# Activation halves side by side, a start offset for the weights, and two matmuls in place of three in the feed-forward part

## The chip, the cores and the metric

The kernel runs on one core of one Trainium2 chip. The metric is the device time of one execution in microseconds. Before the change it is 1631.69 us, the median of three runs (1628.85 to 1634.49).

## The reference

One token sequence of 256 positions and 2048 channels goes through two blocks in fp32. The first has a gated chunk attention and a linear recurrence between two large projections. The second has pooling, latent attention and attention to a memory, and ends in a gated feed-forward part with a short causal convolution over the positions. That last part is what matters here:

```
def conv_glu_ffn(h, w_gate, w_up, conv_w, conv_b, w_down):   # h: 256 x 2048
    g = h @ w_gate                                            # 2048 x 5632
    gp = jnp.pad(g, ((0, 0), (CONV_WIDTH - 1, 0), (0, 0)))
    gc = conv_b
    for j in range(CONV_WIDTH):
        gc = gc + conv_w[j] * gp[:, j:j + S]
    return (jax.nn.silu(gc) * (h @ w_up)) @ w_down            # 5632 x 2048
```

## The kernel before

Activations stand transposed: 128 channels on the partitions, 256 positions (T) along the row. Each fp32 operand of a large product is split into a rounded part and the rest, both as fp32r ("hi" and "lo"). A product is the sum of three matmuls: hi by hi, hi by lo, lo by hi.

Weights come by DMA in tiles of 1 MB (`load`, three buffers `wr`) and are split on the chip by `split_w`: ScalarE writes the high part `wh` (L114, three buffers), VectorE the rest `wl` (L115, two buffers), four 128-row slices at a time where the tile is 256 columns wide. What `split_w` gives is one job of `tile_mm`. A job is put in a short queue (`submit`, one job deep in the feed-forward phase), so that the split of the next job is issued before the matmuls of this one. After its matmuls a job takes steps from the queue of evacuations (`drain`); in the feed-forward phase the budget is 0.1, so one step with a cost is taken per job.

`one` issues the matmuls of one block, a 128 x 128 piece of weights. In mode "T" the weights are the stationary operand and an activation row of 256 positions is the moving one:

```
trip = ((hi[:, s], xh), (hi[:, s], xl), (lo[:, s], xh))
for i, (l, r) in enumerate(trip):
    PE.matmul(o, l, r, start=st and i == 0, stop=sp and i == 2, skip_group_check=True)
```

Two neighbouring blocks share one PSUM bank of 512 columns. In mode "N" the activations are stationary and 512 (or 384, 320) weight columns move.

The feed-forward part takes 22 pairs j of 256 gate and 256 up columns, each with 16 slices of 128 channels and two blocks per slice: 22 x 2 x 16 x 2 = 1408 blocks, four jobs of 8 blocks for gate and four for up. `ev_gate` scales a bank by R3 (L1275), convolves (L1279 to L1281) and applies silu (L1284, L1285). `ev_up` multiplies (L1300) and splits into the tile `f` (L119, L120). Then `w_down` follows, 8 groups x 44 slices x 2 = 704 blocks, with `ev_out` adding the bank to the residual (L1320) and sending it out (L1321). `h1`, `h2` and `h3` hold the normalised inputs of the large products, with all high halves in front of all low halves; `y` tiles hold the mixers' outputs as separate tiles for high and low, `s1` to `s4` the halves of the memory.

Tiles are placed one behind the other in steps of 32 bytes. By that count the weight tiles `wr`, `wh` and `wl` start at byte 32 modulo 128 in each partition, `h` at 0, `y`, `f`, `s1` to `s4` and `qlH` at 96, `kvH` at 0.

Of the kernel before, what the change touches and what calls it, by code (L numbers as in the profile page):

```python
# [17 lines left out]
P = 128  # L18
T = 256
# [39 lines left out]
def trunk_kernel(ctx, tc, a, out):  # L59
# [74 lines left out]
    def tile_mm(src, kc0, kt, cw, mode, banks, act, first, last, pre=None, post=None):  # L134


        raw = load(src, kt, cw)
        n = 2 if mode == "N" else cw // P
        nk = 4 if cw == 256 else 2

        def one(kc, b, hi, lo):
            xh, xl = act(kc0 + kc)
            hi, lo = hi[:, kc % nk, :], lo[:, kc % nk, :]
            st, sp = first and kc == 0, last and kc == kt - 1
            if mode == "T":
                o = banks[b // 2][:, (b % 2) * T : (b % 2) * T + T]
                s = slice(b * P, b * P + P)
                trip = ((hi[:, s], xh), (hi[:, s], xl), (lo[:, s], xh))
                st = st and b % 2 == 0
            else:  # L150
                o = banks[b][:, :cw]
                s = slice(b * P, b * P + P)
                trip = ((xh[:, s], hi), (xh[:, s], lo), (xl[:, s], hi))
            for i, (l, r) in enumerate(trip):
                PE.matmul(o, l, r, start=st and i == 0, stop=sp and i == 2, skip_group_check=True)  # L155
# [127 lines left out]
    def ytile(tag, dt=F32):  # L283
        return yp.tile([P, 8, T], dt, tag=tag, name=tag)

    xt = [ytile("yL0"), ytile("yL1")]
    ada_raw = [ytile(t).rearrange("p (k a) t -> p k (a t)", k=4) for t in ("yH0", "yH1")]
# [126 lines left out]
    def make_h(j):  # L414
        if not h1:
            h = hpool.tile([P, 2, DC, T], F32R, tag="h", name="h1")
            h1.extend((h[:, 0], h[:, 1]))
        V.scalar_tensor_tensor(gs[:, 4 * j : 4 * j + 4], modT[:, 16 + 4 * j : 20 + 4 * j], 1.0,
                               colr("norm_g", 4 * j, 4), ALU.add, ALU.mult)
        for k in range(4 * j, 4 * j + 4):  # L420
            x, H, L, sh = xt[k // 8][:, k % 8, :], h1[0][:, k, :], h1[1][:, k, :], modT[:, k : k + 1]
# [4 lines left out]
    acth = lambda kc: (h1[0][:, kc, :], h1[1][:, kc, :])  # L426

    def front():
        steps = ada_steps((4, 0), ("VVVV", "VPPP"))
        for i, n in enumerate(FRONT):  # L430
# [14 lines left out]
            (lambda kg: a["w_mem_kv"][1, kg], 512, "N", ev_memv)], range(4), lambda kc: (mH(kc), mL(kc)),  # L445
# [350 lines left out]
    def after(kg, n, banks, ng, mode, dst, g, fin):  # L796
        for i, b in enumerate(banks):
            later(0.6, lambda i=i, b=b: part(kg, ng, mode, dst, g, b, i, fin), evq)
        if n == 0:
            steps.append(ada_steps((4 + kg + 1, kg + 1), PAIR) if kg < 3 else gates)  # L800
        if (n % 4 < EARLY and (kg < 3 or n >= GSTART)):
            next(steps[-1], None)
        if kg == 1 and n == 2:
            load_masks()
        if kg == 3 and n == 3:
            when(("in8", "in9", "in10", "in11"), recurrence_inputs)
        if kg == 3 and n in (8, 11):
            i = (n - 8) // 3
            when((f"aq{4 * i}", f"aq{4 * i + 2}", f"ak{4 * i}", f"ak{4 * i + 2}", f"in{4 + i}"), lambda: chunk_heads(i))
        if kg < 3 and n == 11:  # L810
            for _ in steps[-1]:
                pass
            make_h(kg + 1)
            if kg == 2:
                hgt.extend((ytile("yH0"), ytile("yL0")))
# [36 lines left out]
    acty = lambda kc: tuple(t[:, kc % 8, :] for t in y[kc // 8])  # L852

    def gate(src, z, h, k):
        V.tensor_tensor(src[:, h, :], src[:, h, :], z[0][:, h, :], ALU.mult)
        if h == 0:
            y[k // 8] = tuple(ytile(f"{t}{k // 8}", F32R) for t in ("yH", "yL"))
        split(src[:, h, :], *acty(k))
        done.add(f"y{k}")
# [22 lines left out]
    x1s, h2, sq1, pools = [], [], [], []  # L882

# [3 lines left out]
    def ev_x1(g):  # L887
        def one(i, b):
# [3 lines left out]
            gsplit(j, "g_mix", x1s[0][:, j, :], h2[0][:, j, :], h2[1][:, j, :])  # L892
# [9 lines left out]
    def need_y(kg):  # L902
# [6 lines left out]
        if kg == 1 and not xp:  # L909
# [11 lines left out]
            h = hpool.tile([P, 2, DC, T], F32R, tag="h", name="h2")  # L921
            h2.extend((h[:, 0], h[:, 1]))
# [6 lines left out]
    x1, (h2H, h2L) = x1s[0], h2  # L929
# [15 lines left out]
    act2 = lambda kc: (h2H[:, kc, :], h2L[:, kc, :])  # L945
    two = lambda b: b.rearrange("p (a b) -> p a b", a=2)
# [9 lines left out]
    y2p, y2m = ytile("yL0", F32R), ytile("yL1", F32R)  # L956
    y2pH, y2pL, y2mH, y2mL = y2p[:, 0:4, :], y2p[:, 4:8, :], y2m[:, 0:4, :], y2m[:, 4:8, :]
# [146 lines left out]
    y2H, y2L = ytile("yH0", F32R), ytile("yH1", F32R)  # L1104
# [93 lines left out]
    actq = lambda kc: (qlH[:, kc, :], qlL[:, kc, :])  # L1198
    actkv = lambda kc: (kvH[:, kc, :], kvL[:, kc, :])
# [10 lines left out]
    def acty2(kc):  # L1210
        if kc < 4:
            return y2pH[:, kc, :], y2pL[:, kc, :]
        if kc < 12:
            return y2H[:, kc - 4, :], y2L[:, kc - 4, :]
        return y2mH[:, kc - 12, :], y2mL[:, kc - 12, :]

    h3, sq2 = [], []

    def ev_x2(g):
        def one(i, b):  # L1220
            if not h3:
                h = hpool.tile([P, 2, DC, T], F32R, tag="h", name="h3")
                h3.extend((h[:, 0], h[:, 1], h))
                sq2.append(s2("pab", [P, 8, T]))
            s = slice(4 * g + 2 * i, 4 * g + 2 * i + 2)
            V.tensor_tensor(x1[:, s, :], two(b), x1[:, s, :], ALU.add)
            for j in range(s.start, s.stop):
                gsplit(j, "g_ffn", x1[:, j, :], h3[0][:, j, :], h3[1][:, j, :])
                done.add(f"f{j}")
# [30 lines left out]
    def open_f():  # L1260
# [9 lines left out]
    act3 = lambda kc: (h3[0][:, kc, :], h3[1][:, kc, :])  # L1270

    def ev_gate(j, sg):
        def start(b, gp):
            G.memset(gp[:, :, 0:2], 0.0)  # L1274
            V.tensor_tensor(gp[:, :, 2:], two(b), bc(R3, 2), ALU.mult)  # L1275
# [11 lines left out]
        def ev(banks):  # L1287
# [3 lines left out]
            later(0.8, lambda: start(banks[0], gp), evq)  # L1291
# [5 lines left out]
    def ev_up(j, sg):  # L1297
        def one(b):
            t = tmp([P, 2, T], "ub")
            V.tensor_tensor(t, two(b), sg[0], ALU.mult)  # L1300
            split(t, f[j][:, 0], f[j][:, 1])

        def ev(banks):
            later(1.2, lambda: one(banks[0]), evq)
        return ev

    for j in range(FC // 2):
        sg = []
        linear([(lambda kg: a["w_gate"][j, kg], 256, "T", ev_gate(j, sg))], range(2), act3, kt=8,
               need=lambda kg, j=j: need3(j, kg))  # L1310
        linear([(lambda kg: a["w_up"][j, kg], 256, "T", ev_up(j, sg))], range(2), act3, kt=8)
# [16 lines left out]
    for g in range(8):  # L1328
        linear([(lambda kg: a["w_down"][g][:, 2 * kg : min(2 * kg + 2, FC // 4)], 256, "T", ev_out(g))], range((FC + 7) // 8),
# [101 lines left out]
```

## Time and profile before

| | us |
|---|---|
| median of three runs | 1631.69 |
| the profiled execution, device time | 1628.03 |
| its span in the profile | 1626.2 |
| TensorE matmul busy | 1567.1 (96%) |
| VectorE busy | 1122.7 (69%) |
| ScalarE busy | 833.7 (51%) |
| GpSimd busy | 324.0 (20%) |

Matmuls are pipelined, and a matmul's record is longer than the time until the next one starts. So a busy share near 100% says only that matmuls follow each other without a gap; the pace is read from starts: how many matmuls lie in a stretch.

### The profile page before, as it was taken

The numbers are of one execution on the slowest core, as the hardware profiler recorded it, in microseconds if no ns is written. First come the engines' busy times: TensorE is split into PE (matmuls) and PEld (weight loads), VectorE is DVE, ScalarE is ACT, GpSimd is POOL, SyncE is SP. The second block draws the span as 40 slices with busy tenths as digits, with TensorE's granted clock in tenths as the row PEclk, the third lists the DMA queues.
The fourth block names the chain that finished last, engine by engine and source line by source line (L and its number), as shares of the span: only waits on it lengthen the run. The fifth ranks groups of instructions, "written<-read, shape, count | busy, mean of one in ns | idle before, by whom it ended". The sixth has DMA issues, their size and how long they took to land.

```text
span 1626.2 us, 28877 instructions
## 1 busy us (share of the span) xinstructions
PE 1567.1 (96%) x11866; PEld 1492.6 (92%) x11866; DVE 1122.7 (69%) x1476; ACT 833.7 (51%) x1144; POOL 324.0 (20%) x297
## 2 busy tenths in 40 slices
PE   5789999999899999999999999999999999999999
PEld 4677988878899999888999999999999999999999
DVE  7876999899997778568667666656665665444443
ACT  6376555564556645467555544444444444433332
POOL 3533434057643012513001000000000000000000
PEclk9899999999999999999999999999999999999999
DMA  9568888544666576444344554555555555555553
GB/s 387 218 235 309 332 292 310 181 156 156 209 214 205 170 273 240 153 166 142 142 144 182 181 182 182 185 192 186 189 184 181 186 181 191 205 186 213 208 188 130
DMA packets 50964, 332.01 MB, mean 204 GB/s; under 512 B 5648, under 2 KB 8080, under 8 KB 13456
## 3 DMA queue, kind: packets, MB, share of 16 engines
q1 hardware_dynamic: 50832, 330.17, 56.3%
q8 instruction: 93, 1.52, 0.4%
q14 instruction: 39, 0.32, 0.1%
HBM read 328.05 MB, written 2.10 MB: 203 GB/s over the span
## 4 chain that ended last, share of the span: by engine, by line
PE 84%; DVE 8%; DMA 2%; ACT 2%; POOL 2%; issue 2%; SPq 0%; DVEq 0%; ACTq 0%; POOLq 0%
PE mm L155 78%; DVE wl L115 3%; DVE acc L367 1%; POOL acc L373 1%; PE ax L709 1%; ACT wh L114 1%; DMA wr<-in_w_mem_kv_dram 1%; PE ax L382 1%; PE ax L507 1%; PE ax L243 1%; DMA wr<-in_w_out_dram 0%; DVE yH L710 0%; PE ax L499 0%; DVE s L299 0%; PE ax L213 0%
## 5 line engine op out<-in xcount | busy, mean ns | idle before, releaser
L115 DVE TENSOR_TENSOR wl<-wr,wh 128x1024 fp32r<-128x1024 f32 (+2 forms) x516 | 678.2, 1316 | 357.1 <-PE mm L155 316.1
L114 ACT CAST wh<-wr 128x1024 fp32r<-128x1024 f32 (+2 forms) x516 | 536.2, 1043 | 604.7 <-PE mm L155 559.7
L155 PE MATMUL mm<-h,wh 128*128 128x256 f32 x3968 | 712.0, 282 | 0.5 <-ACT wh L114 0.5
L155 PEld LDWEIGHTS mm<-h,wh 128*128 128x128 f32 x3968 | 611.1, 189 | 1.5 <-ACT wh L114 1.1
L155 PE MATMUL mm<-h,wl 128*128 128x256 f32 x1984 | 560.1, 282 | 8.1 <-DVE wl L115 8.0
L155 PEld LDWEIGHTS mm<-h,wl 128*128 128x128 f32 x1984 | 375.3, 189 | 10.1 <-DVE wl L115 9.9
L155 PE MATMUL mm<-f,wh 128*128 128x256 f32 x1408 | 239.4, 276 | 0.0
L155 PE MATMUL mm<-wh,h 128*128 128x512 f32 (+1 forms) x704 | 222.3, 391 | 0.0
L155 PEld LDWEIGHTS mm<-f,wh 128*128 128x128 f32 x1408 | 212.2, 188 | 0.0
L155 PE MATMUL mm<-f,wl 128*128 128x256 f32 x704 | 194.5, 276 | 0.0
L155 PEld LDWEIGHTS mm<-wh,h 128*128 128x128 f32 x704 | 131.1, 188 | 27.7
L155 PE MATMUL mm<-wl,h 128*128 128x512 f32 (+1 forms) x352 | 137.1, 389 | 3.3 <-DVE wl L115 3.3
L155 PEld LDWEIGHTS mm<-f,wl 128*128 128x128 f32 x704 | 132.2, 188 | 0.0
L155 PE MATMUL mm<-yH,wh 128*128 128x256 f32 x512 | 117.9, 283 | 0.7 <-ACT wh L114 0.7
L155 PE MATMUL mm<-yL,wh 128*128 128x256 f32 x512 | 117.7, 281 | 0.0
L155 PE MATMUL mm<-yH,wl 128*128 128x256 f32 x384 | 106.9, 280 | 1.7 <-DVE wl L115 1.7
L373 POOL TENSOR_TENSOR acc<-acc,pts 128x512 f32<-128x512 f32 x45 | 75.6, 1680 | 110.0 <-ACT pts L372 94.5
L155 PEld LDWEIGHTS mm<-yH,wh 128*128 128x128 f32 x512 | 87.0, 188 | 1.0 <-ACT wh L114 0.9
L155 PEld LDWEIGHTS mm<-yL,wh 128*128 128x128 f32 x512 | 87.3, 189 | 0.0
L155 PEld LDWEIGHTS mm<-wl,h 128*128 128x128 f32 x352 | 66.2, 188 | 19.3 <-DVE wl L115 5.9
L1274 POOL MEMSET gp<- 128x4 f32 x22 | 2.2, 102 | 400.6 <-DVE sg L1281 398.6
L155 PEld LDWEIGHTS mm<-yH,wl 128*128 128x128 f32 x384 | 72.4, 189 | 2.4 <-DVE wl L115 2.3
(306 smaller groups left out, 1622.1 us busy)
## 6 DMA issues: line engine op xcount, KB each, us to landing
wr<-in_w_in_dram SPq DMA_DIRECT2D x76, 1024.0 KB, 4.8
wr<-in_w_gate_dram SPq DMA_DIRECT2D x44, 1024.0 KB, 4.8
wr<-in_w_up_dram SPq DMA_DIRECT2D x44, 1024.0 KB, 4.9
wr<-in_w_down_dram SPq DMA_DIRECT2D x40, 1024.0 KB, 4.8
yH<-in_w_ada_dram SPq DMA_DIRECT2D x28, 1024.0 KB, 7.3
wr<-in_w_ada_dram SPq DMA_DIRECT2D x16, 1024.0 KB, 4.9
wr<-in_w_out_dram SPq DMA_DIRECT2D x16, 1024.0 KB, 4.9
wr<-in_w_o_dram SPq DMA_DIRECT2D x16, 1024.0 KB, 4.9
```

Source lines behind the costliest of these rows:

```text
L114: S.copy(hi, raw[:, k : k + n, :])
L115: V.tensor_tensor(lo, raw[:, k : k + n, :], hi.bitcast(F32), ALU.subtract)
L155: PE.matmul(o, l, r, start=st and i == 0, stop=sp and i == 2, skip_group_check=True)
L243: PE.transpose(ps[:, j * T + tb * P : j * T + tb * P + P], d[:, j, tb * P : tb * P + P], ident)
L367: V.scalar_tensor_tensor(accs[0], raw[:, k, :], cc, accs[0], ALU.mult, ALU.add)
L373: G.tensor_tensor(accs[1], accs[1], t, ALU.add)
L382: PE.matmul(ps[:, j * P : j * P + P], acc[:, j * P : j * P + P], ones, start=i == 0, stop=i == len(accs) - 1, skip_group_check=True)
L507: PE.matmul(po[:, :T], vblk(0), t[:, :T], start=True, stop=False, skip_group_check=True)
L709: PE.matmul(ps[:, j, b, :], k2[:, j, s], q2[:, j, s], start=True, stop=True)
L1274: G.memset(gp[:, :, 0:2], 0.0)
```

## The change

- All tiles of activation halves now hold each slice's high and low half side by side ([slice, half, 256]), so that both are one run of 512 columns. `h1`, `h2`, `h3`, `y`, `f` and the second block's mixer outputs are laid out so; the four `y` tags become two of double size.
- Small unused tiles shift addresses: 64 bytes ahead of `wh`, 64 bytes ahead of `wl`, 32 in the pool of `h`, 32 in the pool of `y`, 32 in the pool of `f`. By the count of sizes the activation tiles then start at byte 32 modulo 128, `wh` at 96, `wl` at 32 as before, `kvH` at 64.
- A mode "T2" in the whole feed-forward part: per block one matmul of 512 columns (high weights by both halves) and one of 256 (low weights by the high half). Each block has a bank of its own, whose two halves must be added when it is evacuated. The evacuations go by block (256 positions) instead of by pair of blocks. The multiplication by R3 moves from VectorE to GpSimd.

```diff
     def split_w(raw, k, cw):
         n = 4 if cw == 256 else 2
+        if not padded:
+            padded.append(wpool.tile([P, 16], F32, tag="pada", name="pada", bufs=1))
         hi = wpool.tile([P, n, cw], F32R, tag="wh", name="wh", bufs=3)
+        if len(padded) == 1:
+            padded.append(wpool.tile([P, 16], F32, tag="padb", name="padb", bufs=1))
         lo = wpool.tile([P, n, cw], F32R, tag="wl", name="wl", bufs=2)
...
+            elif mode == "T2":
+                s = slice(b * P, b * P + P)
+                trip = ((two(banks[b]), hi[:, s], xx), (banks[b][:, :T], lo[:, s], xh))
...
+    hpool.tile([P, 8], F32, tag="pad1", name="pad1")
...
+    yp.tile([P, 8], F32, tag="pad2", name="pad2")
...
-            h = hpool.tile([P, 2, DC, T], F32R, tag="h", name="h1")
-            h1.extend((h[:, 0], h[:, 1]))
+            h1.append(hpool.tile([P, DC, 2, T], F32R, tag="h", name="h1"))
...
+        fp.tile([P, 8], F32, tag="pad2", name="pad2")
...
-        def start(b, gp):
-            G.memset(gp[:, :, 0:2], 0.0)
-            V.tensor_tensor(gp[:, :, 2:], two(b), bc(R3, 2), ALU.mult)
+        def start(k, b, gp):
+            G.memset(gp[:, 0:2], 0.0)
+            s = sg[0][:, k, :]
+            S.copy(s, b[:, T:])
+            V.tensor_tensor(s, b[:, :T], s, ALU.add)
+            G.tensor_tensor(gp[:, 2:], s, R3, ALU.mult)
...
-            later(0.8, lambda: start(banks[0], gp), evq)
+            for k, b in enumerate(banks):
+                later(0.4, lambda k=k, b=b: start(k, b, gp[:, k, :]), evq)
...
-        def one(b):
-            t = tmp([P, 2, T], "ub")
-            V.tensor_tensor(t, two(b), sg[0], ALU.mult)
-            split(t, f[j][:, 0], f[j][:, 1])
+        def one(k, b):
+            t = tmp([P, T], "ub")
+            S.copy(t, b[:, T:])
+            V.tensor_tensor(t, b[:, :T], t, ALU.add)
+            V.tensor_tensor(t, t, sg[0][:, k, :], ALU.mult)
+            split(t, f[j][:, k, 0, :], f[j][:, k, 1, :])
...
-            later(1.2, lambda: one(banks[0]), evq)
+            for k, b in enumerate(banks):
+                later(1.0, lambda k=k, b=b: one(k, b), evq)
...
-        def one(b):
-            c = slice(2 * g, 2 * g + 2)
-            V.tensor_tensor(x1[:, c, :], two(b), x1[:, c, :], ALU.add)
-            SP.dma_start(out[:, c, :], x1[:, c, :])
+        def one(k, b):
+            c = 2 * g + k
+            V.tensor_tensor(x1[:, c, :], b[:, T:], x1[:, c, :], ALU.add)
+            V.tensor_tensor(x1[:, c, :], b[:, :T], x1[:, c, :], ALU.add)
+            if k:
+                SP.dma_start(out[:, c - 1 : c + 1, :], x1[:, c - 1 : c + 1, :])
```

## Rows read from the trace of the kernel before

**Rows 1.** The page's parts 1 and 4: engines, and the chain by line.
```profile
PE 1567.1 (96%) x11866; PEld 1492.6 (92%) x11866; DVE 1122.7 (69%) x1476; ACT 833.7 (51%) x1144; POOL 324.0 (20%) x297
...
PE mm L155 78%; DVE wl L115 3%; DVE acc L367 1%; POOL acc L373 1%; PE ax L709 1%; ACT wh L114 1%; DMA wr<-in_w_mem_kv_dram 1%; PE ax L382 1%; PE ax L507 1%; PE ax L243 1%; DMA wr<-in_w_out_dram 0%; DVE yH L710 0%; PE ax L499 0%; DVE s L299 0%; PE ax L213 0%
```
**Rows 2.** Windows: inside the gate and up products, inside the down product.
```profile
core 0: us, PE busy (x) PEld busy (x) DVE busy (x) ACT busy (x) POOL busy (x), PEclk, DMA share, GB/s
898.00:1380.00 482.00, 482.00 (x4076) 482.00 (x4075) 294.07 (x319) 225.62 (x256) 31.37 (x42) 1.00 0.52 185
1400.00:1619.00 219.00, 219.00 (x1935) 219.00 (x1934) 102.96 (x88) 83.77 (x80) 0.00 (x0) 1.00 0.55 194
```
**Rows 3.** Chain of waits in time: start us, us, what (feed-forward; mixers' output product; 320 columns).
```profile
579.27 17.91 PE mm L155 x158
...
562.87 2.83 PE mm L155 x24
...
695.56 3.52 PE mm L155 x24
...
894.62 727.88 PE mm L155 x6240
```
**Rows 4.** Timeline, TensorE, 512 columns, stationary h: start us, us, instruction.
```profile
148.12 0.39 PE L155 MATMUL mm<-wl,h 128*128 128x512 f32 x1
...
156.52 0.40 PE L155 MATMUL mm<-wl,h 128*128 128x512 f32 x1
```
**Rows 5.** Timeline, TensorE, 512 columns, stationary s: 16 matmuls from first to last start.
```profile
43.14 0.39 PE L155 MATMUL mm<-wl,s 128*128 128x512 f32 x1
...
46.81 0.40 PE L155 MATMUL mm<-wh,s 128*128 128x512 f32 x1
```
**Rows 6.** Groups by line and form, VectorE and ScalarE: count, busy us, mean ns, idle before.
```profile
L120 DVE TENSOR_TENSOR f<-ub,f 128x512 fp32r<-128x512 f32 x22 | 15.1, 684 | 0.0
L119 ACT CAST f<-ub 128x512 fp32r<-128x512 f32 x22 | 13.5, 615 | 0.0
L855 DVE TENSOR_TENSOR s<-s,s 128x256 f32<-128x256 f32 x16 | 7.3, 474 | 1.5 <-ACT s L644 1.5
L120 DVE TENSOR_TENSOR yL<-s,yH 128x256 fp32r<-128x256 f32 x16 | 7.2, 453 | 1.5 <-ACT yH L119 0.7
L119 ACT CAST yH<-s 128x256 fp32r<-128x256 f32 x16 | 6.2, 404 | 4.0 <-DVE s L855 4.0
L996 DVE TENSOR_TENSOR yH<-ax,yH 128x256 fp32r<-128x256 f32 x8 | 3.3, 416 | 0.0
L1119 ACT COPY heads<-mm 128x256 f32<-128x256 f32 x8 | 3.0, 376 | 0.0
L971 POOL TENSOR_TENSOR z<-pab,z 128x256 f32<-128x256 f32 x4 | 3.0, 738 | 0.2
```
**Rows 7.** Timeline, VectorE then GpSimd, inside one pair of the gate and up products.
```profile
1008.25 0.69 DVE L1275 TENSOR_TENSOR gp<-mm,R 128x512 f32<-128x512 f32 x1 [1.56 <-PE mm L155]
...
1011.17 1.22 DVE L115 TENSOR_TENSOR wl<-wr,wh 128x1024 fp32r<-128x1024 f32 x1
...
1014.00 1.98 DVE L115 TENSOR_TENSOR wl<-wr,wh 128x1024 fp32r<-128x1024 f32 x1 [1.21 <-PE mm L155]
...
1019.66 0.69 DVE L1300 TENSOR_TENSOR ub<-mm,sg 128x512 f32<-128x512 f32 x1 [1.61 <-PE mm L155]
...
1013.60 1.30 POOL L1285 TENSOR_TENSOR sg<-sg,R 128x512 f32<-128x512 f32 x1 [0.56 <-ACT sg L1284]
```
**Rows 8.** Chain of waits, the end of the kernel: start us, us, what.
```profile
1615.00 7.49 PE mm L155 x66
1622.49 0.02 issue
1622.52 0.69 DVE x L1320
```

More of the change, by code (lines that the diff above doesn't have):

```diff
@@ L141, in one @@
         def one(kc, b, hi, lo):
-            xh, xl = act(kc0 + kc)
+            xh, xl, xx = act(kc0 + kc)
             hi, lo = hi[:, kc % nk, :], lo[:, kc % nk, :]
@@ L152, in one @@
                 s = slice(b * P, b * P + P)
-                trip = ((xh[:, s], hi), (xh[:, s], lo), (xl[:, s], hi))
-            for i, (l, r) in enumerate(trip):
-                PE.matmul(o, l, r, start=st and i == 0, stop=sp and i == 2, skip_group_check=True)
+                trip = ((o, xh[:, s], hi), (o, xh[:, s], lo), (o, xl[:, s], hi))
+            for i, (d, l, r) in enumerate(trip):
+                PE.matmul(d, l, r, start=st and i == 0, stop=sp and i == len(trip) - 1, skip_group_check=True)
         def job(k, hi, lo):
@@ L254, in bc, with two @@
         return ap.unsqueeze(1).to_broadcast([P, n, ap.shape[-1]])
+    def two(ap):
+        return ap.rearrange("p (a b) -> p a b", a=2)
     def flat(ap):
@@ L281, in slot, with ytile @@
         return sp_.tile(shape, dt, tag=tag, name=tag)
[L283 to L287, printed above, removed]
+    def ytile(tag, shape=(2, 8), dt=F32):
+        return yp.tile([P, *shape, T], dt, tag=tag, name=tag)
+    xt, ada_raw = zip(*((t[:, 0], t[:, 1].rearrange("p (k a) t -> p k (a t)", k=4)) for t in (ytile("y0"), ytile("y1"))))
     memwork = hpool.tile([P, 2, DC, T], F32, tag="h", name="memwork")
@@ L420, in make_h @@
         for k in range(4 * j, 4 * j + 4):
-            x, H, L, sh = xt[k // 8][:, k % 8, :], h1[0][:, k, :], h1[1][:, k, :], modT[:, k : k + 1]
+            x, H, L, sh = xt[k // 8][:, k % 8, :], h1[0][:, k, 0, :], h1[0][:, k, 1, :], modT[:, k : k + 1]
             V.scalar_tensor_tensor(x, x, gs[:, k : k + 1], R2, ALU.mult, ALU.mult)
@@ L424, in make_h @@
             V.scalar_tensor_tensor(L, x, sh, H.bitcast(F32), ALU.add, ALU.subtract)
-    acth = lambda kc: (h1[0][:, kc, :], h1[1][:, kc, :])
+    pair_of = lambda t, k: (t[:, k, 0, :], t[:, k, 1, :], t[:, k, :, :])
+    acth = lambda kc: pair_of(h1[0], kc)
     def front():
@@ L444, in trunk_kernel @@
     linear([(lambda kg: a["w_mem_kv"][0, kg], 512, "N", ev_memk),
-            (lambda kg: a["w_mem_kv"][1, kg], 512, "N", ev_memv)], range(4), lambda kc: (mH(kc), mL(kc)),
+            (lambda kg: a["w_mem_kv"][1, kg], 512, "N", ev_memv)], range(4), lambda kc: (mH(kc), mL(kc), None),
            ahead=load_mem, aside=front(), done_loads=lambda: token_R(sums[:, 0:4, :], None, rm))
@@ L814, in after @@
             if kg == 2:
-                hgt.extend((ytile("yH0"), ytile("yL0")))
+                t = ytile("y0")
+                hgt.extend((t[:, 0], t[:, 1]))
     for kg in range(4):
@@ L851, in trunk_kernel @@
     y = {}
-    acty = lambda kc: tuple(t[:, kc % 8, :] for t in y[kc // 8])
+    acty = lambda kc: pair_of(y[kc // 8], kc % 8)
     def gate(src, z, h, k):
@@ L856, in gate @@
         if h == 0:
-            y[k // 8] = tuple(ytile(f"{t}{k // 8}", F32R) for t in ("yH", "yL"))
-        split(src[:, h, :], *acty(k))
+            y[k // 8] = ytile(f"y{k // 8}", (8, 2), F32R)
+        split(src[:, h, :], *acty(k)[:2])
         done.add(f"y{k}")
@@ L882, in trunk_kernel @@
     x1s, h2, sq1, pools = [], [], [], []
+    act2 = lambda kc: pair_of(h2[0], kc)
     def blk(banks, i):
@@ L891, in one @@
             V.scalar_tensor_tensor(x1s[0][:, j, :], b, modT[:, 32 + j : 33 + j], x1s[0][:, j, :], ALU.mult, ALU.add)
-            gsplit(j, "g_mix", x1s[0][:, j, :], h2[0][:, j, :], h2[1][:, j, :])
+            gsplit(j, "g_mix", x1s[0][:, j, :], *act2(j)[:2])
             done.add(f"h{j}")
@@ L920, in need_y @@
                 SP.dma_start(x1s[0][:, 4 * j : 4 * j + 4, :], a["xT"][:, 4 * j : 4 * j + 4, :])
-            h = hpool.tile([P, 2, DC, T], F32R, tag="h", name="h2")
-            h2.extend((h[:, 0], h[:, 1]))
+            h2.append(hpool.tile([P, DC, 2, T], F32R, tag="h", name="h2"))
     wo = lambda g: (lambda kg: a["w_out"][g, kg], 512, "T", ev_x1(g))
@@ L928, in trunk_kernel @@
     finish()
-    x1, (h2H, h2L) = x1s[0], h2
+    x1 = x1s[0]
     s2 = lambda tag, shape, dt=F32: pools[0].tile(shape, dt, tag=tag, name=tag)
@@ L944, in trunk_kernel @@
             G.tensor_tensor(rtab[:, w, i], cs[:, c], bc(gro[:, w, x, :], 4), ALU.mult)
-    act2 = lambda kc: (h2H[:, kc, :], h2L[:, kc, :])
-    two = lambda b: b.rearrange("p (a b) -> p a b", a=2)
     def scaled(dst):
@@ L953, in scaled @@
         return f
-    y2p, y2m = ytile("yL0", F32R), ytile("yL1", F32R)
-    y2pH, y2pL, y2mH, y2mL = y2p[:, 0:4, :], y2p[:, 4:8, :], y2m[:, 0:4, :], y2m[:, 4:8, :]
+    y2pm = ytile("y0", (8, 2), F32R)
+    y2pH, y2pL, y2mH, y2mL = y2pm[:, 0:4, 0, :], y2pm[:, 0:4, 1, :], y2pm[:, 4:8, 0, :], y2pm[:, 4:8, 1, :]
     pz, pab = s2("z4", [P, 4, T]), s2("pab", [P, 8, T])
@@ L1101, in trunk_kernel @@
         ensure(f"y2{j}")
-    y2H, y2L = ytile("yH0", F32R), ytile("yH1", F32R)
+    y2 = ytile("y1", (8, 2), F32R)
+    y2H, y2L = y2[:, :, 0, :], y2[:, :, 1, :]
     heads = hpool.tile([P, 2, DC, T], F32, tag="h", name="heads")
@@ L1196, in latent_heads @@
             attend_end()
-    actq = lambda kc: (qlH[:, kc, :], qlL[:, kc, :])
-    actkv = lambda kc: (kvH[:, kc, :], kvL[:, kc, :])
+    actq = lambda kc: (qlH[:, kc, :], qlL[:, kc, :], None)
+    actkv = lambda kc: (kvH[:, kc, :], kvL[:, kc, :], None)
     kvu = lambda i, mode, evac: linear([(lambda kg: a["w_kv_up"][i], 512, mode, evac)], range(1), actkv, kt=2)
@@ L1210, in acty2 @@
     def acty2(kc):
[L1211 to L1215, printed above, removed]
+        return pair_of(y2, kc - 4) if 4 <= kc < 12 else pair_of(y2pm, kc if kc < 4 else kc - 8)
     h3, sq2 = [], []
+    act3 = lambda kc: pair_of(h3[0], kc)
     def ev_x2(g):
@@ L1221, in one @@
             if not h3:
-                h = hpool.tile([P, 2, DC, T], F32R, tag="h", name="h3")
-                h3.extend((h[:, 0], h[:, 1], h))
+                h3.append(hpool.tile([P, DC, 2, T], F32R, tag="h", name="h3"))
                 sq2.append(s2("pab", [P, 8, T]))
@@ L1227, in one @@
             for j in range(s.start, s.stop):
-                gsplit(j, "g_ffn", x1[:, j, :], h3[0][:, j, :], h3[1][:, j, :])
+                gsplit(j, "g_ffn", x1[:, j, :], *act3(j)[:2])
                 done.add(f"f{j}")
@@ L1308, in trunk_kernel @@
         sg = []
-        linear([(lambda kg: a["w_gate"][j, kg], 256, "T", ev_gate(j, sg))], range(2), act3, kt=8,
+        linear([(lambda kg: a["w_gate"][j, kg], 256, "T2", ev_gate(j, sg))], range(2), act3, kt=8,
                need=lambda kg, j=j: need3(j, kg))
-        linear([(lambda kg: a["w_up"][j, kg], 256, "T", ev_up(j, sg))], range(2), act3, kt=8)
+        linear([(lambda kg: a["w_up"][j, kg], 256, "T2", ev_up(j, sg))], range(2), act3, kt=8)
     finish()
     flush()
-    actf = lambda kc: (f[kc // 2][:, 0, kc % 2, :], f[kc // 2][:, 1, kc % 2, :])
+    actf = lambda kc: pair_of(f[kc // 2], kc % 2)
     def ev_out(g):
-        def one(b):
-            c = slice(2 * g, 2 * g + 2)
-            V.tensor_tensor(x1[:, c, :], two(b), x1[:, c, :], ALU.add)
-            SP.dma_start(out[:, c, :], x1[:, c, :])
+        def one(k, b):
[4 more added lines that the diff above has]
+                SP.dma_start(out[:, c - 1 : c + 1, :], x1[:, c - 1 : c + 1, :])
         def ev(banks):
-            later(0.8, lambda: one(banks[0]), evq)
+            for k, b in enumerate(banks):
+                later(0.8, lambda k=k, b=b: one(k, b), evq)
         return ev
@@ L1328, in trunk_kernel @@
     for g in range(8):
-        linear([(lambda kg: a["w_down"][g][:, 2 * kg : min(2 * kg + 2, FC // 4)], 256, "T", ev_out(g))], range((FC + 7) // 8),
+        linear([(lambda kg: a["w_down"][g][:, 2 * kg : min(2 * kg + 2, FC // 4)], 256, "T2", ev_out(g))], range((FC + 7) // 8),
                actf, kt=8, nkc=FC)
```

4 lines of the change are left out of this document (2 added, 2 removed).

## The prediction

> **What bounds the kernel now.** I read the page first: TensorE's matmuls are 78% of the chain that ended last, all at L155, and the feed-forward part, which the change rewrites, is the chain's longest unbroken piece, 727.88 us [rows 1, 3]. In there nothing waits: 6240 matmuls follow each other on the chain, VectorE is busy 294 of 482 us, ScalarE 226, the DMA about half, and the granted clock is 1.00, the 2.4 GHz level [rows 2, 3]. So the stage costs the number of its matmuls times their pace, and the pace is to be read from counts. In the gate and up products 482.00 us hold 4076 matmuls of 256 columns: 118.3 ns each. In the down product 219.00 us hold 1935 of the same shape: 113.2 ns [rows 2]. A block of three costs 354.8 ns in the one and 339.5 in the other. Shape, engines' work per matmul and clock don't tell these two apart; what differs is where the moving operand starts (h at byte 0 modulo 128, f at 96, the weights at 32 in both).
>
> The other stages complete the picture. The mixers' output products move `y`, at 96 like f, and show both paces with nothing between: 158 matmuls in 17.91 us (113.4 ns) and 24 in 2.83 us (117.9 ns) [rows 3]. So 96 against 32 permits the fast pace, and what happened before (a stall, another product in between) decides whether it is taken; `h` at 0 shows the slow one alone. With 512 weight columns moving (byte 32), 36 matmuls take 8.40 us from start to start, 233.3 ns, where the stationary operand stands at 0 [rows 4], and 16 take 3.67 us, 229.4 ns, where it stands at 96 [rows 5]. With 320 columns it is 3.52 us for 24, 146.7 ns [rows 3]. From 320 to 512: 86.6 ns for 192 columns, 0.451 ns per column, and 2.4 ns per matmul that don't depend on the columns. For 256 columns that line gives 117.9 ns, just the slow pace. So the slow pace is the ordinary one of these operands, 0.451 ns per column where 2.4 GHz would be 0.417, and the fast one is an exception to it.
>
> **The feed-forward matmuls.** Two matmuls for three leave the 768 columns of a block as they are and take one matmul's fixed cost, 2.4 ns, from each of 1408 + 704 blocks: 5.1 us. All else hangs on the pace at the new addresses. No row has 512 columns from activations, nor low weights (32) against a moving operand at 32; the high ones (96 against 32) have the distance of 64 that f and `y` have, and just the two places of rows 5 with the roles exchanged. The bounds:
> - all at the slow pace: 233.3 + 117.9 = 351.2 ns. Gate and up 1408 x (351.2 - 354.8) = -5.1 us, down 704 x (351.2 - 339.5) = +8.2 us: +3.1 us.
> - 512 columns as in rows 5: 229.4 + 113.2 = 342.6 ns. -17.2 and +2.2: -15.0 us.
> - all at the fast pace: 339.5 ns. -21.5 us and 0.
> - one column per cycle of the granted 2.4 GHz: 768 / 2.4 = 320 ns. -49.0 and -13.7: -62.7 us; no row allows less.
>
> I take the fast pace, -21.5 us: it is the row nearest in distance and it was held for the whole down product, and in the down product neither ScalarE's nor VectorE's work broke it.
>
> A rule of the Trainium skill speaks against so much. "TensorE: Matmul & The Clock Gate", section "Wait — 56ns, not 53.3ns?", gives N/2.4 + 2.5 ns from start to start for matmuls in a row at the full clock, and its section "Step-by-step: what each phase is for" says that loading the next weights takes no read bandwidth from the running matmul. By it neither a weight load less nor an address changes the pace, and merging is worth about 2.5 ns per block. The trace agrees on the constant (2.4 ns) and not on the rest: 113.2 and 118.3 ns stand at one shape [rows 2]. What it would make of the time is the rival "no effect of the place" below.
>
> **The products ahead of it.** Their instructions stay, their addresses move. 1728 matmuls move `h` (118.3 to 113.2: at best -8.8 us), 1536 move `y` (some half slow: -3.5 to +3.5), 960 move 512 weight columns past `h` (233.3 to 226.4 at best: -6.6), 192 past `s` (at worst +0.7): -18.9 to +4.2 us. By the chain's 78%, 1268 us, less 739 for the feed-forward part (1408 x 354.8 + 704 x 339.5 ns), some 530 us of these products are on the path, in short pieces between waits for VectorE, ScalarE and the DMA, whose ends they don't move [rows 1]. I take -6 us. The four `y` tags becoming two costs nothing: the halves that now share a tile were taken and freed together before, and the second block takes its tiles after the last product that reads the old ones.
>
> **The evacuations.** Per pair, gate loses one VectorE instruction of 690 ns and gains two adds out of PSUM of 416; up loses 690 and 684 and gains twice 416 + 474 + 453 (nearest shapes): +1.45 us [rows 6, 7]. GpSimd gains two multiplications of 738 ns, and where GpSimd works the split of the weights took 1.98 us in place of 1.22 [rows 6, 7], so up to 2 x 0.75 more. VectorE goes from 61% of 22.7 us, 13.8 us, to 16.8 of 21.7 us, 77%. ScalarE: 10.6 us + four copies of 376 + two casts of 404 - 615 = 12.3 us, 57% [rows 2, 6]. Beside TensorE both still fit. What can show is one late split: `wl` has two buffers, so each split must lie inside one job of 8 blocks, 2.72 us. An up step now has 416 + 474 + 453 ns with a ScalarE cast of 404 in the middle; with the split's 1.22 that is 2.97 us, 0.25 too many if VectorE sits through the cast, and two such jobs follow each other. Behind a late split TensorE waits at its second matmul. Ends: 0 and 22 x 0.5 = 11 us. I take 2 us, near nothing, since VectorE's order already puts splits between the steps of one evacuation. The chain copy, add, multiply, convolve, silu is longer, but its result is needed only when the up product ends, four jobs later. Two banks per product make three products in the six banks; a gate's banks are read in the two jobs after it and wanted again eight jobs later, 21.7 us: nothing. In the down product VectorE is at 47% [rows 2] and hides four adds of 416 per group. At the very end the last matmul is followed by 0.69 us of VectorE [rows 8], and now by two adds, 0.83: +0.1; the bank ahead of it is done earlier. SP issues the same DMAs, 5% closer together, over a queue that is half busy.
>
> **Sum.** -21.5 - 6 + 2 + 0.1 = -25.4 us on the profiled execution's 1628.03 (span 1626.2 and 1.8 around it): 1602.6 us. The median stands 3.7 us above that execution; I set the forecast between, at 1605 us.
>
> **Rivals.**
> - Full pace. The two places were a good pair by luck of the start in rows 3; with the right places the excess per column goes altogether: 320 + 2 x 2.4 = 324.8 ns. Gate and up -42.2, down -10.3, with the rest as above -56: 1575 us. For it: the excess comes and goes at one shape, so it isn't the array's own. Against it: no row is below 113.2.
> - No effect of the place: each stage keeps its pace per column, -5.1 for the fixed cost, +2.1 for the evacuations, nothing ahead of it: 1625 us, or 1628 by the median. For it: `y` has both paces at one place. Against it: `h` never has the fast one.
> - The slow pace everywhere, the other side. Low weights and moving operand at the same byte 32 spoil the start of each matmul of 256, and the down product loses the pace that it has by luck: +3.1, ahead of it +4.2, evacuations +2.1, so +9: 1638 us. It decides for slower when the block in the down product passes 351 ns and gate and up gain under 6.
> - VectorE bound. The pace improves, but the splits come late: with 11 us in place of 2 it is 1614, and at 1.1 us per pair the whole gain is gone, 1628.
> - That the tiles don't land where intended: by the count of sizes they do, so I fold it into the second.
>
> **How the numbers follow.** Forecast 0.48 (its own range 1592 to 1616), full pace 0.20, no effect of the place 0.10, slow everywhere 0.16, VectorE bound 0.06. About 0.3%, 5 us, is what a measurement of this kernel can tell from no change. Faster: 0.48 + 0.20 + half of the last = 0.71; same: 0.10 + 0.03 = 0.13; slower 0.16. The range goes from 1570, into the full pace, to 1636, into the slow case, and leaves out a part of each.
>
> **What would show it.** In the changed kernel, windows inside gate and up and inside down should hold 2 matmuls per 340 ns: 5.9 per us, against 5.7 at the slow pace and 6.2 at the full one; both stages alike. No idle time of TensorE behind L115 or L114 (now `wl`, `wh`) in the feed-forward part, above all in the two jobs after an up product; VectorE near 77%, ScalarE near 57% there. The 24-matmul pieces of `h` and `y` ahead of it should take 2.72 us in place of 2.83. The prediction is wrong in its main step if the block takes over 346 ns or under 333, and in its second if the part ahead of the feed-forward part gets more than 15 us shorter, or longer.

## The result, and the profile after

The changed kernel takes 1610.64 us (median of four runs, 1608.93 to 1611.15), the kernel before 1631.22 beside it: 0.988 of it, 95% interval 0.987 to 0.989. The forecast was 1605 with a range of 1570 to 1636. The profiled execution took 1608.93 us with a span of 1607.2, so 19.0 us less span than before.

The page's parts 1 and 4 of the changed kernel, to be held against [rows 1]; L165 is the old L155, L121 the old L115:

```profile
PE 1549.3 (96%) x9754; PEld 1391.6 (87%) x9754; DVE 1157.4 (72%) x1610; ACT 860.0 (54%) x1254; POOL 366.9 (23%) x363
...
PE mm L165 78%; DVE wl L121 4%; DVE acc L382 2%; POOL acc L388 1%; PE ax L724 1%; DMA wr<-in_w_mem_kv_dram 1%; PE ax L397 1%; ACT wh L120 1%; DMA wr<-in_w_ada_dram 1%; PE ax L253 1%; PE ax L522 1%; PE ax L223 0%; PE ax L514 0%; DVE s L314 0%; PE ax L650 0%
```

TensorE's share and the share of its matmuls on the chain have not moved: a faster pace doesn't show in a busy share. It shows in counts. The windows of the changed kernel inside gate and up and inside down, columns as in [rows 2]:

```profile
898.00:1360.00 462.00, 462.00 (x2720) 408.69 (x2719) 321.13 (x426) 252.94 (x363) 75.96 (x106) 1.00 0.55 194
1366.00:1600.00 234.00, 234.00 (x1379) 207.31 (x1378) 117.33 (x116) 89.61 (x86) 0.00 (x0) 1.00 0.57 192
```

Two matmuls make a block now: 462.00 us for 1360 blocks are 339.7 ns and 234.00 for 689.5 are 339.4, both 340.0 from first to last start. Before it was 354.8 and 339.5 [rows 2]. So gate and up came to where the down product had been all along, and the down product stayed. Weight loads (second column) fell from 100% of the stretch to 88%.

The chain of the changed kernel in time, with the pieces that answer to [rows 3] (start us, us, what):

```profile
579.50 20.16 PE mm L165 x171
...
563.10 2.83 PE mm L165 x24
...
696.67 3.50 PE mm L165 x24
...
704.09 8.43 PE mm L165 x36
...
895.97 707.23 PE mm L165 x4160
```

The feed-forward piece holds the same 2080 blocks as the 6240 matmuls of before and takes 707.23 us in place of 727.88: 20.65 us less. It begins at 895.97, 1.35 us later than before, and behind it 0.3 us were added: 20.65 - 1.35 - 0.3 = 19.0, the whole difference of the spans. Ahead of it nothing was won: the mixers' output product, which had a stretch at 113.4 ns per matmul, is at 117.9 in the stretch that answers to it (171 in 20.16 us) as in all others (24 in 2.83), and 512 weight columns take 234.2 ns (36 in 8.43 us).

The groups of the changed kernel between 898 and 1360 us (count, busy us, mean ns, idle before):

```profile
L165 PE MATMUL mm<-h,wh 128*128 128x512 f32 x1360 | 462.4, 389 | 0.0
L165 PE MATMUL mm<-h,wl 128*128 128x256 f32 x1360 | 375.5, 276 | 0.0
...
L121 DVE TENSOR_TENSOR wl<-wr,wh 128x1024 fp32r<-128x1024 f32 x170 | 211.0, 1241 | 106.6 <-PE mm L165 102.5 <-ACT wh L120 1.2
...
L1294 DVE SCALAR_TENSOR_TENSOR sg<-gp,cols,sg 128x256 f32<-128x256 f32 x44 | 28.8, 655 | 0.8
...
L1293 DVE SCALAR_TENSOR_TENSOR sg<-gp,cols,sg 128x256 f32<-128x256 f32 x44 | 21.0, 477 | 9.2 <-ACT sg L1292 9.2
L1316 DVE TENSOR_TENSOR ub<-ub,sg 128x256 f32<-128x256 f32 x42 | 17.9, 425 | 2.9
L126 DVE TENSOR_TENSOR f<-ub,f 128x256 fp32r<-128x256 f32 x42 | 17.7, 422 | 1.0
L1315 DVE TENSOR_TENSOR ub<-mm,ub 128x256 f32<-128x256 f32 x42 | 17.7, 421 | 10.1 <-ACT ub L1314 10.1
L1287 DVE TENSOR_TENSOR sg<-mm,sg 128x256 f32<-128x256 f32 x42 | 17.6, 418 | 10.1 <-ACT sg L1286 10.1
```

The idle time ahead of TensorE's matmuls is 0.0 in both groups: no split came late. VectorE is busy 321 of 462 us, 70%, ScalarE 253, 55%. The end of the chain of the changed kernel, for [rows 8]:

```profile
1595.93 7.27 PE mm L165 x43
1603.20 0.02 issue
1603.22 0.43 DVE x L1337
1603.66 0.02 issue
1603.68 0.42 DVE x L1338
```

Two adds of 0.43 and 0.42 us stand where one of 0.69 stood.

### The profile page after: what moved, and what is told of

It is laid out like the page before. It is cut to its first block, busy times and chain, and to the rows that moved or that the text cites. A ratio compares the mean times of both kernels' runs of the same rounds, so it can differ in the third digit from the quotient of the medians.

```text
span 1607.2 us, 24896 instructions
## 1 busy us (share of the span) xinstructions
PE 1549.3 (96%) x9754; PEld 1391.6 (87%) x9754; DVE 1157.4 (72%) x1610; ACT 860.0 (54%) x1254; POOL 366.9 (23%) x363
## 4 chain that ended last, share of the span: by engine, by line
PE 83%; DVE 9%; POOL 2%; issue 2%; ACT 2%; DMA 1%; SPq 0%; DVEq 0%; ACTq 0%; POOLq 0%
PE mm L165 78%; DVE wl L121 4%; DVE acc L382 2%; POOL acc L388 1%; PE ax L724 1%; DMA wr<-in_w_mem_kv_dram 1%; PE ax L397 1%; ACT wh L120 1%; DMA wr<-in_w_ada_dram 1%; PE ax L253 1%; PE ax L522 1%; PE ax L223 0%; PE ax L514 0%; DVE s L314 0%; PE ax L650 0%
## 5 line engine op out<-in xcount | busy, mean ns | idle before, releaser
L121 DVE TENSOR_TENSOR wl<-wr,wh 128x1024 fp32r<-128x1024 f32 (+2 forms) x516 | 669.6, 1299 | 346.7 <-PE mm L165 308.9
L165 PE MATMUL mm<-h,wh 128*128 128x512 f32 (+1 forms) x2560 | 691.4, 343 | 0.4 <-ACT wh L120 0.4
L165 PE MATMUL mm<-h,wl 128*128 128x256 f32 x1984 | 553.5, 279 | 7.5 <-DVE wl L121 7.3
L165 PEld LDWEIGHTS mm<-h,wh 128*128 128x128 f32 x2560 | 444.1, 189 | 56.6 <-ACT wh L120 1.0
L165 PEld LDWEIGHTS mm<-h,wl 128*128 128x128 f32 x1984 | 374.2, 189 | 9.5 <-DVE wl L121 9.3
L165 PE MATMUL mm<-f,wh 128*128 128x512 f32 x704 | 239.4, 389 | 0.0
L165 PE MATMUL mm<-wh,h 128*128 128x512 f32 (+1 forms) x704 | 222.1, 391 | 0.0
L165 PE MATMUL mm<-f,wl 128*128 128x256 f32 x704 | 194.4, 276 | 0.0
L165 PE MATMUL mm<-y,wh 128*128 128x256 f32 x1024 | 185.3, 283 | 0.0
L165 PEld LDWEIGHTS mm<-y,wh 128*128 128x128 f32 x1024 | 156.6, 188 | 0.3 <-ACT wh L120 0.3
L165 PEld LDWEIGHTS mm<-wh,h 128*128 128x128 f32 x704 | 131.2, 188 | 29.1
L165 PEld LDWEIGHTS mm<-f,wh 128*128 128x128 f32 x704 | 132.1, 188 | 27.3
L165 PE MATMUL mm<-y,wl 128*128 128x256 f32 x512 | 143.9, 282 | 2.6 <-DVE wl L121 2.6
L165 PE MATMUL mm<-wl,h 128*128 128x512 f32 (+1 forms) x352 | 137.8, 392 | 3.4 <-DVE wl L121 3.4
L165 PEld LDWEIGHTS mm<-f,wl 128*128 128x128 f32 x704 | 132.2, 188 | 0.0
L1288 POOL TENSOR_TENSOR gp<-sg,R 128x256 f32<-128x256 f32 x44 | 35.9, 818 | 314.3 <-DVE sg L1287 314.3
L165 PEld LDWEIGHTS mm<-y,wl 128*128 128x128 f32 x512 | 96.0, 188 | 3.4 <-DVE wl L121 3.4
L165 PEld LDWEIGHTS mm<-wl,h 128*128 128x128 f32 x352 | 66.3, 188 | 18.7 <-DVE wl L121 5.9
L165 PE MATMUL mm<-wh,s 128*128 128x512 f32 x128 | 45.4, 435 | 10.2 <-ACT wh L120 10.2
L634 DVE TENSOR_TENSOR s<-mm,s 128x512 f32<-128x512 f32 x72 | 49.0, 680 | 2.1 <-PE mm L165 1.8
```

Of the source, the lines that this page charges most:

```text
L165: PE.matmul(d, l, r, start=st and i == 0, stop=sp and i == len(trip) - 1, skip_group_check=True)
L634: V.tensor_tensor(d, b, d, ALU.add)
L1288: G.tensor_tensor(gp[:, 2:], s, R3, ALU.mult)
```

## The experiments

The question left by the result: what gave gate and up the pace of the down product? Theory A: the merging. Theory B: the places. Theory C: both are needed. First TensorE alone, then three kernels that each do one part.

**m1, TensorE alone at many places.** The program writes one act tile and two weight tiles and runs streams of blocks, each place twice; m, h and l are added to bases that are multiples of 128 bytes. A short wait for a ScalarE copy stands ahead of each stream. Core of it:

```
for kind, m, h, l, gap in _configs():            # x, H, L: act slice, high, low weights at these bytes
    for r in range(ROUNDS):                       # 2
        ...                                       # a small matmul, and one that waits for its ScalarE copy
        for i in range(n):
            ...
            if kind == "pair":
                PE.matmul(bk[b], H, act[:, x : x + 512], ...)
                PE.matmul(bk[b][:, :T], L, act[:, x : x + T], ...)
```

> TensorE alone: nothing of the reference is computed here, the output is zeros and a few sums. One stream of 48 blocks after another, each twice, with a short wait for ScalarE ahead of it. 'pair' is a 512- and a 256-column matmul per block, 'three' three of 256; m, h, l are the bytes modulo 128 at which the moving halves, the high and the low weights start, g the columns from high to low half. Theory A (merging makes the pace): every pair stream takes 340 ns per block whatever the places, the three streams 340 to 355. Theory B (the places make it): only some places give 340, for pair and three alike, m32 h96 l32 among them; the others 351 to 355. Theory C (both are needed): pair at m32 h96 l32 takes 340, other pairs 351, and three streams mostly 353. If a stall decides between two paces, the two rounds of one stream differ.

Measured, from start to start in the settled part of each stream: the pairs take 346.7 to 353.3 ns per block, the threes 340.0 to 363. The pair at the changed kernel's places, m32 h96 l32, takes 350.0 in both rounds. 340.0 appears only with three matmuls at m96 h32 l32, and there in all six rounds, whatever the distance from high to low half (1, 2 or 16 KB). No pair took 340.0 at any of the 21 places tried. In the first round of the pair at m32 h96 l32 every 512-column matmul is on the chain of that run; between these two lie 40 blocks in 14.00 us:

```profile
264.37 0.23 PE pair_m_h_l_g256x L122
...
278.37 0.23 PE pair_m_h_l_g256x L122
```

This speaks against A and against C as I had put it: the pair at the new places was not fast here, and places alone were, but others.

**e1, merging without the places.**

```diff
-        if not padded:
-            padded.append(wpool.tile([P, 16], F32, tag="pada", name="pada", bufs=1))
...
-    hpool.tile([P, 8], F32, tag="pad1", name="pad1")
...
-        fp.tile([P, 8], F32, tag="pad2", name="pad2")
```

> The changed kernel without its five small unused tiles: pairs side by side and two matmuls per block, but h at byte 0, y and f at 96, both weights at 32. Theory A (merging makes the pace): 340 ns per block in gate, up and down, about 1610 us. Theory B or C (the places are needed): gate and up at 233.3 + 118 = 351 ns, 1408 x 11 = 15.5 us more, about 1626 us; down at 340 (96 against 32 has the distance of 64) or 351, then 8 us more.

Measured: 1638.72 us, 1.0049 of before (1.003 to 1.0068). 353.3 ns per block in gate, up and down alike. The distance of 64 bytes that f has in the down product did not help: it lost the 340 it had with three matmuls.

**e2, the places without merging.** The changed kernel with before's `ev_gate`, `ev_up`, `ev_out` and, here for up and in the same way for gate and down,

```diff
-        linear([(lambda kg: a["w_up"][j, kg], 256, "T2", ev_up(j, sg))], range(2), act3, kt=8)
+        linear([(lambda kg: a["w_up"][j, kg], 256, "T", ev_up(j, sg))], range(2), act3, kt=8)
```

> The changed kernel's layout and places, but three matmuls of 256 per block in the feed-forward part and the evacuations of before. Theory A: gate and up stay near 353 to 355 ns per block and down at 340 to 353, so 1630 to 1640 us. Theory B (the places make the pace): 340 ns in all three, about 1610 us. Theory C: 353 in all three, 1408 x 13.4 + 704 x 13.4 = 28 us above the changed kernel, about 1639 us; the mixers' output products of the changed kernel, three matmuls at these places and all at 117.8 ns, speak for this one.

Measured: 1638.09 us, 1.0054 of before (1.0039 to 1.0069), and 353.3 ns in all three products.

**e3, h at byte 96 modulo 128 with three matmuls.**

```diff
+    hpool.tile([P, 24], F32, tag="pad1", name="pad1")
```

and 32 bytes ahead of `y` and of `f`, so that these keep their place modulo 128.

> The kernel before with one edit: h starts at byte 96 modulo 128 as f and y do, all else at its old place, three matmuls. If 96 against 32 is what gave the down product its 113.2 ns, gate and up fall from 355 to 340 ns per block, 1408 x 15 = 21 us, about 1610 us, and merging is not needed. If the pace there is a matter of how the stream began (y shows both at 96), gate and up stay at 353, about 1629 us, or show both paces in stretches.

Measured: 1636.95 us, 1.0051 of before (1.0036 to 1.0066). Gate and up at 353.3, and the down product too, although f stood at 96 as before: it had moved by 128 bytes. So the place modulo 128 does not fix the pace; whether the rest of the address or the start does, this run can't say. The same unbroken piece of the chain, 2080 blocks, in e1, e2 and e3:

```profile
898.88 734.91 PE mm L161 x4160
```

```profile
898.26 734.95 PE mm L165 x6240
```

```profile
896.50 734.94 PE mm L155 x6240
```

Three different edits, one length: 353.3 ns.

**m2, TensorE alone at the kernels' own addresses.** Buffers alternate as in the kernels (three `wh`, two `wl`, 16 slices).

```
("a_after_gate_x", "pair", 73632, 2048, 1024, 43616, 55968, 16),      # act, step, high to low, wh, wl, slices
("f_before_down_x", "three", 106720, 1024, 2048, 43552, 55840, 2),
...
("l_after_act_a_x", "pair", 73760, 2048, 1024, 43616, 55968, 16),          # act 128 further; m_ and n_ 256 and 512
```

> TensorE alone again (nothing of the reference is computed), now with the very addresses, buffers and orders of the kernels run so far: streams of 48 blocks, three times each after waits of different length. If the addresses alone fix the pace, a_ and b_ (the changed kernel's gate and down) take 340 ns per block, c_ and d_ (old places, two matmuls) 353, e_ 355 and f_ 340 (the kernel before), g_ and h_ 353 (new places, three matmuls), i_ and k_ 353 (h at 96). l_ to p_ shift one operand of a_ by a multiple of 128 bytes: at 340 the place modulo 128 is all that counts. If what comes ahead of the stream decides, the rounds of one stream differ, or a_ and b_ miss 340 as pair_m32_h96_l32 did in the first measurement (350). q_ (the y tiles of before) showed both paces in the kernel.

Each wait is a small matmul that needs a ScalarE copy. In the trace the second and the third one stand behind three or four of the stream's own matmuls, and no matmul has idle time ahead of it, so a "start" here is a slightly different mix of instructions. Measured, ns per block after one, two and three waits:

| stream | one | two | three | in the kernel |
|---|---|---|---|---|
| a_ changed, gate | 340.0 | 350.0 | 340.0 | 340.0 |
| b_ changed, down | 340.0 | 350.0 | 340.0 | 340.0 |
| c_, d_ old places, pair | 353.1 to 353.4 | | | 353.3 |
| e_ before, gate | 354.9 | 354.9 | 355.1 | 355.0 |
| f_ before, down | 340.0 | 340.0 | 340.0 | 340.0 |
| g_, h_ new places, three | 353.3 to 353.5 | | | 353.3 |
| i_, k_ of e3 | 353.3 | 353.3 | 340.0 | 353.3 |
| l_ act 128 further | 349.8 | 350.0 | 350.0 | |
| m_, n_ act 256, 512 further | 340.0 | 350.0 | 340.0 | |
| o_ low weights 128 further | 346.7 | 346.7 | 346.7 | |
| p_ high weights 128 nearer | 350.0 | 340.0 | 340.0 | |
| q_ y of before | 353.3 | 340.0 | 340.0 | 353 and 340 |

The chain of this run, the long pieces of a_ (90, 93 and 90 matmuls) and of l_ (start us, us, what):

```profile
22.95 15.30 PE a_after_gate_x L143 x90
...
40.54 16.22 PE a_after_gate_x L143 x93
...
58.36 15.31 PE a_after_gate_x L143 x90
...
537.30 16.81 PE l_after_act_a_x L143 x96
```

45 blocks in 15.30 us are 340.0 ns, and 46.5 in 16.22 are 349: one program, one address, two paces. So three things are shown at once. TensorE alone has the paces of the kernels: from b_ on next to no other engine works beside it (a_'s first round ran ahead of its wait, while ScalarE still filled the operands). The addresses say which paces a stream took in its three rounds: shifts of the activations by 256 and 512 bytes change nothing, while one of 128 does. And where a stream has more than one pace, the start decides: b_, m_ and n_ all have 340.0, 350.0, 340.0 after the same three starts. The pair's 350.0 in m1 is the other one of these two. At e3's own addresses (i_, k_) the third start gave 340.0, so e3's 353.3 was a matter of its start too.

**e4, e5, e6: the parts of the placing.** f 128 bytes further; the weights' two unused tiles taken out; the activations' three taken out.

```diff
-        fp.tile([P, 8], F32, tag="pad2", name="pad2")
+        fp.tile([P, 40], F32, tag="pad2", name="pad2")
```

> The changed kernel with f 128 bytes further on (same place modulo 128, all else unmoved). If the place modulo 128 is what counts: 340 ns per block in the down product, 1610 us. If the whole address counts, or the distance to the weights: down at 346 to 353 ns, 4 to 9 us more; gate and up stay at 340 in both.

> The changed kernel without the two unused tiles among the weights: activations at 32, high and low weights at 32. If the high weights' place is needed: about 352 ns per block (the first measurement's pair_m32_h32_l32), 2112 x 12 = 25 us more, 1636 us. If the activations' place alone does it: 340 ns, 1610 us.

> The changed kernel without the three unused tiles among the activations: high weights at 96, low at 32, h at 0, y and f at 96. If the weights' place alone does it: 340 ns per block, 1610 us. If both are needed: 347 to 349 ns in gate and up and in down (the first measurement's pair_m0_h96 and pair_m96_h96), 16 to 19 us more, about 1628 us.

Measured (one run each, before at 1632.13 beside them): e4 1618.7 us, gate and up at 340.0, down at 350.0, as l_ had shown. e5 1624.17 us, 346.8 and 346.7: 8.0 us below before, where I had expected either 352 or 340.0. e6 1635.67 us, gate and up 353.2, where I had expected 347 to 349, down 346.7. The long pieces of the three chains:

```profile
898.69 714.28 PE mm L165 x4160
```

```profile
897.35 721.09 PE mm L161 x4160
```

```profile
899.65 730.25 PE mm L165 x4160
```

e6 moves activations alone and loses 340.0 in all three products, so the weights' offset by itself does not give it here; e4 moves f alone by 128 bytes and loses it in the down product. e5 does not show by itself that the weights' offset is needed: by the count of sizes its edit moves the high weights by 64 bytes, but the low weights and all activations behind them by 128, and 128 bytes alone change the pace (l_, o_).

**e7, h moved, no merging.** The kernel before with h at byte 224 modulo 256, the place of f; the two small tiles make `y` and f move by 256 bytes, so that they keep theirs:

```diff
+    hpool.tile([P, 56], F32, tag="pad1", name="pad1")
...
+    yp.tile([P, 8], F32, tag="pad2", name="pad2")
...
+        fp.tile([P, 8], F32, tag="pad2", name="pad2")
```

> The kernel before, three matmuls and its old layout, with one thing changed: h starts at byte 224 modulo 256 (e3 had it at 96 modulo 256), where f, y and the streams with 340 ns in all their rounds stand. If the whole place modulo 256 is what counts: 340 ns per block in gate, up and down without any merging, 1408 x 15 = 21 us less than before; the products ahead of it that move h or hold it stationary also gain (1728 matmuls at 113.3 in place of 118.3, 960 at 228.9 in place of 233.3), up to 13 us of which about half shows: 1600 to 1607 us, below the changed kernel. If merging is needed for gate and up after all: 353 ns there, 1625 to 1630 us.

Measured in five rounds: 1603.77 us (1602.91 to 1608.00), 0.9838 of before (0.9822 to 0.9855): faster than the changed kernel, whose interval begins at 0.987. Gate, up and down are at 340.0 with three matmuls per block. The windows inside gate and up and inside down of e7:

```profile
898.00:1350.00 452.00, 452.00 (x3991) 452.00 (x3989) 291.37 (x311) 219.70 (x249) 28.76 (x40) 1.00 0.55 194
1362.00:1590.00 228.00, 228.00 (x2014) 228.00 (x2013) 106.55 (x92) 88.21 (x85) 0.00 (x0) 1.00 0.58 197
```

452.00 us for 3991 matmuls are 113.3 ns each. Weight loads fill 452 of 452 us here and 409 of 462 in the changed kernel, and a block takes 340.0 in both: the third weight load cost nothing. The long piece of e7's chain,

```profile
890.80 707.24 PE mm L155 x6240
```

is as long as the changed kernel's 707.23, and starts 5.2 us earlier: ahead of it h's products were at 113.3 ns in most stretches and the 512 weight columns past h at 229.

**e8, does the start decide in the kernel?** The changed kernel with small matmuls that wait for ScalarE put into gate and up, two of them in one place and three in another:

```diff
+        if j in (7, 14) and kg == 0:
+            tick = r3t
+            for _ in range(2 if j == 7 else 3):
+                tk = bank("ax")
+                PE.matmul(tk[:, :P], tick[0], ones, start=True, stop=True, skip_group_check=True)
+                S.copy(tick[1], tk[:, :P])
+                tick.reverse()
```

> The changed kernel with TensorE made to wait for ScalarE twice ahead of pair 7 and three times ahead of pair 14 of gate and up, some 1 to 2 us each time. If how a stream starts decides between its two paces, as in the streams a_ and b_ (340, 350, 340 after one, two and three waits), the blocks go from 340 to 350 ns behind one of the two, 64 blocks x 10 ns per pair: up to 5 us for the pairs 7 to 13. If the kernel's other work holds the pace at 340, nothing changes behind the waits.

Measured: 1626.04 us in one run. The chain of e8 (start us, us, what):

```profile
899.36 141.46 PE mm L165 x832
1040.82 0.22 PE ax L1271 x2
1041.04 1.05 PE mm L165 x6
1042.09 0.40 PE ax L1271 x2
1042.49 151.32 PE mm L165 x890
...
1196.33 423.98 PE mm L165 x2423
```

832 matmuls in 141.46 us and 890 in 151.32 are 340.0 ns per block; after the three waits at 1194 us, 2423 in 423.98 are 350.0, to the end of the down product. The inserted matmuls themselves add 0.6 and 0.9 us to the chain; the other pace cost some 12 (1211 blocks x 10 ns). In m2 it was the second start that gave 350.0 and the third 340.0; here two left the pace alone and three changed it. So a start decides, but m2 does not tell which start does what in the kernel.

## Why the prediction was right

**What bounds the kernel.** Held. The stage is matmuls times pace, nothing waits in it, and the change of pace alone accounts for it: 20.65 us less in that piece, where the whole span fell by 19.0.

**The feed-forward matmuls.** The term held to the tenth: 340.0 for the expected 339.5 ns per block, both stages alike, gate and up some 21 us shorter (-21.5 expected), down 0. The ground I gave for it held only in part. I took the fast pace because the high weights would stand 64 bytes from the moving operand, as f's do. e1's down product and e2 have that distance too and run at 353.3. The pace comes with the whole combination (the address of the moving operand, where 128 bytes count and 256 do not, those of both weights, where 128 count and more was not tried, and whether a block is two matmuls or three) and, where that leaves two paces open, with the start. That the changed kernel's four runs lie within 2.2 us, where the other pace would cost 2112 x 10 ns = 21 us, says that it took the same pace each time. So the number came out for a wrong reason and with luck: that 340.0 is open at these places, and that the kernel's start takes it and not 350.0, followed from nothing in the prediction, and none of m1's pairs had it.

**The ordinary pace by a line through 320 and 512 columns.** It gave 351.2 for a block at the slow pace; 353.3 was measured in e1, e2 and e3. Good for a bound, but one shape has many paces: 340.0, 346.7, 350.0, 353.3 and 355.0 in the kernels, and others between and above in m1, up to 363. The line through two of them is not a law.

**The products ahead of it.** -6 us expected, +1.35 measured on the chain: the one step that failed. By the prediction's own sign (wrong if that part gets longer) this step is wrong. I took some of the fast pace as the likely outcome for three matmuls at the new places; there three matmuls had the slow pace in every run (g_, h_, e2), and `y` lost the stretches at 113.4 that it had. The reading that byte 96 modulo 128 against 32 permits the fast pace stands: f_, i_, k_ and q_ have 340.0 after at least one start. Carrying it over, by the distance of 64 bytes, to activations at 32 and high weights at 96 was the mistake. e7 shows what I had counted on, at another address: its feed-forward piece starts 3.8 us earlier than before's.

**The evacuations.** +2 us expected, 0 measured: no idle time ahead of TensorE. The adds out of PSUM took 418 and 421 ns (416 taken), the multiplication 425 (474 taken), the split of f 422 (453 taken). VectorE came to 70% and not 77% above all because the splits of the weights, for which up to 1.5 us more per pair was put in, got shorter: 1241 ns in the mean, where it was 1315 before (between 1000 and 1300 us), and none took over 1.4 us, where one per pair had taken 1.98 [rows 7]. What GpSimd's new work cost appears elsewhere: L1294 takes 655 ns where L1293, the same form, takes 477. The 21 of its 44 instructions that ran beside GpSimd's L1288 took 848 ns, the 23 others 478. The end cost 0.3 in place of 0.1.

**The sum.** -21.5 - 6 + 2 + 0.1 was expected; -20.65, +1.35, 0 and +0.3 came of it on the chain, and on the profiled execution 19.1 us in place of 25.4.

**The rivals.** "Full pace" is out: no stream of any run had a block under 340.0 ns, which is 816 cycles at the granted 2.4 GHz for 768 columns. "No effect of the place" is out too: e1, the changed kernel without the unused tiles, has 353.3 and takes some 8 us more than before, and the tiles alone separate it from the changed kernel. "Slow everywhere" is what came true in e1, e2 and e3, where the down product lost its pace as described. "VectorE bound" is out, since no matmul waited for a split. The Trainium skill, "TensorE: Matmul & The Clock Gate", section "Wait — 56ns, not 53.3ns?", with N/2.4 + 2.5 ns from start to start would make 325 ns of a block (an estimate). The traces disagree, with 340.0 at the least, and the measurement decides. The Trainium skill, "SBUF — State Buffer", section "Who interferes with whom", says that TensorE waits for no other engine; m2 agrees, since TensorE alone had the kernels' paces, 340.0 to 355.

**What stays open.** What TensorE loses at the slower paces, and by what a start picks one of two. The runs show which addresses and starts have which pace, not why. That the weights' offset is needed by itself is not shown either. Not tried: streams with addresses shifted by less than 32 bytes, or with the matmuls of a block in another order.

## What to carry to other kernels

Read a matmul stage's pace from counts per window, not from busy shares, and if two stages with the same shapes differ, try addresses before rewriting the arithmetic: here a move of h by one unused tile, with two more to keep the other tiles in place, gave more (26.6 us) than the merged matmuls with their offsets and all their new evacuations (20.6 us). Test a place over the whole address (for the activations a shift of 128 bytes was not neutral, one of 256 was) and over several starts, since a stream can keep the pace with which it began for hundreds of us (e8).

## What the runs showed that was not expected

- Matmul streams of fp32r operands settle into a steady pace that differs by address and start: 340.0, 346.7, 350.0, 353.3 or 355.0 ns in the kernels for blocks of 768 columns at a granted clock of 1.00. A few small matmuls in between, 0.9 us in all, can move a stream from one to the other (e8: 340.0 to 350.0 for 424 us).
- One weight load less per block is worth nothing at the same pace: 340.0 with two loads and with three (e7).
- The same addresses and orders give the same paces with and without VectorE, ScalarE, GpSimd and DMA at work beside TensorE (m2 against the kernels: c_ to f_ within 0.2 ns; a_, b_, i_ and k_ in some of their rounds, by the start).
